# Other staging buffers for two weight pieces and for the half results, ahead of the second half of an output projection

## The chip, the cores and the metric

The kernel runs on one core of one Trainium2 chip. A core has a matrix engine (PE in the profile, with its weight loads as PEld), a vector engine (DVE), a scalar engine (ACT), a general engine (POOL) and a synchronising engine (SP), which here only issues DMA transfers. Each engine works through its own list of instructions in order, and waits at the head of that list until what an instruction needs is there. The metric is the time of one execution in microseconds (us) of device time; lower is better. "t0" to "t7" and other short names below are mine; the kernel's own names are given beside them.

## The reference, cut to what matters

One layer, 1024 tokens of width 1024, in float32. Only the first sub-layer's end and the second's start matter here:

```python
y_ssm = s5_mixer(u, ...)                      # 1024 x 512
y_fox = forgetting_attention(q, k, v, ...)    # 1024 x 512, 8 heads of 64
y_mix = concatenate([rms_norm(y_ssm, ssm_out_g), rms_norm(y_fox, fox_out_g)], axis=-1)
x = x + rms_norm(y_mix @ w_out, mix_post_g)
h = rms_norm(x, xa_pre_g)
x = x + rms_norm(memory_cross_attention(h, mem_n, xa_wq, xa_wkv, xa_wo), xa_post_g)
```

The product with `w_out` has two halves: the rows that belong to `y_ssm` and the rows that belong to `y_fox`. The change lies where the second half is computed and added to the first.

## The kernel before, in words

All of the work is one program in which a scheduler sets the order: the instructions are written in program order, with priorities, and the framework's own timeline decides the final order on each engine. Tiles come from pools. A pool with the tag "a" has 2 buffers, "b" 2, "c" 3, "d" and "e" 1 each, `raw` 2, `whl` 3 (`BUFS`, line 193; lines 59 to 66). Each buffer holds 128 x 1024 floats (512 KB); `whl` and `slab` buffers hold a high and a low part. Buffers of a tag are handed out in turn, in program order, so a tile waits for the work on the tile that had its buffer before. Float32 products are made of three matmuls, of a high and a low part (`mm3`, lines 121 to 124); the parts come from `split` (line 113 on ACT makes the high part, line 115 or 117 on DVE the low one).

Around the change, in program order:

* **Attention heads.** The last unit of the attention is head 7. Its values are multiplied (L782, L783), its result `yt` is brought out by ACT (L789) and DVE (L790), split into `yf` (L113, L117), squared (L802) and added up on POOL (L803) into the tile "d"; a few tiny matmuls (L237) turn these sums into one number per token, from which DVE and ACT work out `r_f`, the factor of the norm of `y_fox` (L139 to L145).
* **First half of the projection.** It has been written to DRAM earlier (`t1_d`, shown as `t_d` in the profile).
* **The four pieces of the weights of the second half** (lines 1026 to 1032), 512 KB each: load (L1029) and split into a `slab` (L113, L115). I call them f0 to f3. All four are loaded into `raw` before, which has two buffers.
* **The loop over eight tiles of 128 tokens** (lines 1035 to 1057). Tile j loads 128 rows of `x` into a "c" buffer (L1038), loads the half results into a tile `t` by two transfers of 64 rows each (L1041; I call this tile tj and the two transfers its pair), and for each half of the columns: 12 matmuls into a PSUM bank `x` (L122 to L124; there are four such banks), then on DVE `t = bank * r_f + t` (L1048), on ACT the sums of squares (L1050), on POOL `t = t * g_mp` (L1052). The row `g_mp` is loaded into "d" (L952) once the sums of the heads have been read there. At the end of a tile come the norm (L1054, L139 to L145), `x1 = t * r + x` on DVE (L1056) and the store of x1 from POOL's queue (L1057).
* **Between these**, `build_a(1)` is stepped: it loads four pieces of the query weights (`in_wqT`, L158, I call them q0 to q3) into `raw`, splits them into `whl`, and multiplies them into PSUM banks `g` (L122 to L124 with `e` and `whl`).
* **Next stage** (lines 1204 to 1221): for each of four heads, values from DRAM are split into a "b" tile (L1209), two pieces of `wo` go through `raw` or "e" into `whl`, and 24 matmuls fill four banks, `g` for heads 0 and 2 and `x` for heads 1 and 3. The rest of the second sub-layer follows.

So SP's list holds all the loads, in one order; ACT's list holds splits that wait for loads, and bank evacuations; a load that is late holds up everything that stands behind its split.

The lines around the change in the kernel before:

```python
    BUFS = {"a": 2, "b": 2, "c": 3, "d": 1, "e": 1, "t2": 3, "yt": 2}
...
    for i in range(4):
        w = raw([P, D])
        sp.dma_start(out=w, in_=a["w_out_f"][i])
        hl = slab([P, 2, D])
        split(hl[:, 0], hl[:, 1], w)
        wo.append(hl)
...
        t = tt("aab"[j % 3])
```

Of the kernel before, what the change touches and what calls it, by code (L numbers as in the profile page):

```python
# [17 lines left out]
P = 128  # L18
S = 1024
D = 1024  # L20
# [32 lines left out]
def layer(ctx: ExitStack, tc: tile.TileContext, a, out):  # L53
# [15 lines left out]
    def slab(shape, dt=F32R):  # L69
        return slabp.tile(shape, dt, name="slab", tag="slab")  # L70
# [4 lines left out]
    def raw(shape):  # L75
        return rawp.tile(shape, F32, name="raw", tag="raw")
# [7 lines left out]
    def sm(n, name):  # L84
        return small.tile([P, n], F32, name=name, tag=name)
# [26 lines left out]
    def split(hi, lo, src, mul=None, lo_eng=None):  # L112
        first = act.activation(out=hi, in_=src, func=AF.Copy, scale=1.0 if mul is None else mul)  # L113
        if mul is None:
            (lo_eng or dve).tensor_tensor(out=lo, in0=src, in1=hi.bitcast(F32), op=ALU.subtract)  # L115
        else:
            dve.scalar_tensor_tensor(out=lo, in0=src, scalar=mul, in1=hi.bitcast(F32),  # L117
                                     op0=ALU.mult, op1=ALU.subtract)
        return first

    def mm3(ps, lh, ll, rh, rl, first, last):
        pe.matmul(ps, lh, rh, start=first, stop=False)  # L122
        pe.matmul(ps, lh, rl, start=False, stop=False)  # L123
        pe.matmul(ps, ll, rh, start=False, stop=last)  # L124
# [70 lines left out]
    def tt(tag, shape=None, dt=F32):  # L195
        return t4.tile(shape or [P, S], dt, name=tag, tag=tag, bufs=BUFS[tag])
# [671 lines left out]
    def step(g, n=1):  # L868
        for _ in range(n):
            if next(g, "end") == "end":  # L870
                return
# [151 lines left out]
    def x_ps(shape):  # L1023
        return psx.tile(shape, F32, name="x", tag="x")

    wo = []
    for i in range(4):
        w = raw([P, D])
        sp.dma_start(out=w, in_=a["w_out_f"][i])  # L1029
        hl = slab([P, 2, D])  # L1030
        split(hl[:, 0], hl[:, 1], w)
        wo.append(hl)
    g_mp = gain_row(0, "d")
    a1 = build_a(1)
    for j in range(NT):
        ts = slice(j * P, (j + 1) * P)
        xt = tt("c")
        sp.dma_start(out=xt, in_=a["x"][ts, :])  # L1038
        t = tt("aab"[j % 3])
        for i in range(2):  # L1040
            sp.dma_start(out=t[64 * i:64 * i + 64], in_=t1_d.rearrange("j (k s) d -> s k j d", s=16)[2 * j + i])  # L1041
        ss4, ss, r = sm(4, "ss4"), sm(1, "ss"), sm(1, "r")
        for h in range(2):
            hs = slice(h * 512, h * 512 + 512)
            ps = x_ps([P, 512])
            for k in range(4):
                mm3(ps, yf[k][:, 0, ts], yf[k][:, 1, ts], wo[k][:, 0, hs], wo[k][:, 1, hs], k == 0, k == 3)
            dve.scalar_tensor_tensor(out=t[:, hs], in0=ps, scalar=r_f[:, j:j + 1], in1=t[:, hs], op0=ALU.mult, op1=ALU.add)  # L1048
            for q in range(2 * h, 2 * h + 2):
                act.activation(out=tt("yt", [P, 256]), in_=t[:, q * 256:q * 256 + 256], func=AF.Square,  # L1050
                               accum_out=ss4[:, q:q + 1])
            pool.tensor_tensor(out=t[:, hs], in0=t[:, hs], in1=g_mp[:, hs], op=ALU.mult)  # L1052
            step(a1)
        dve.tensor_reduce(out=ss, in_=ss4, op=ALU.add, axis=mybir.AxisListType.X)  # L1054
        rsqrt_mean(r, ss, D)
        dve.scalar_tensor_tensor(out=xt, in0=t, scalar=r, in1=xt, op0=ALU.mult, op1=ALU.add)  # L1056
        stC.dma_start(out=x1_d[j], in_=xt)  # L1057
# [249 lines left out]
    def ev():  # L1307
        return evp.tile([P, 512], F32, name="ev", tag="ev")
# [111 lines left out]
    for n in range(2):  # L1420
        w = ev()
# [185 lines left out]
```

## Time and profile before

| | |
|---|---|
| median of 3 runs | 1432.37 us (1430.96 to 1433.04) |
| the profiled execution's own time | 1430.57 us |
| its span, first to last instruction | 1428.8 us |
| mean granted clock of the matrix engine | 0.992 |
| PE busy | 1390.7 us (97%) |
| DVE, ACT, POOL busy | 1003.7, 708.0, 410.9 us |
| span from 475 to 585 us | PE busy 97.9 of 110 us |
| span from 585 us to the end | PE busy 834 of 843 us |

The profiled execution took 1.8 us more than its span and 1.8 us less than the median. The stretch of the change lies between about 475 and 585 us of the span, where PE is idle for 12 of 110 us; after it, it is idle for 9 of 843 us. In the timelines, a row has the start in us, the length in us, the engine, the line, the operation with output and input tiles, a count, and in brackets the idle time of the engine ahead of it with what ended it. SPq is SP's list, where a row is the issuing of a transfer, not the transfer. The names there come without numbers: `t_d` in `a<-t_d` is `t1_d`.

### The profile page before, as it was taken

The numbers are of one execution on the slowest core, as the hardware profiler recorded it, in microseconds if no ns is written. First come the engines' busy times: TensorE is split into PE (matmuls) and PEld (weight loads), VectorE is DVE, ScalarE is ACT, GpSimd is POOL, SyncE is SP. The second block draws the span as 40 slices with busy tenths as digits, with TensorE's granted clock in tenths as the row PEclk, the third lists the DMA queues.
The fourth block names the chain that finished last, engine by engine and source line by source line (L and its number), as shares of the span: only waits on it lengthen the run. The fifth ranks groups of instructions, "written<-read, shape, count | busy, mean of one in ns | idle before, by whom it ended". The sixth has DMA issues, their size and how long they took to land.

```text
span 1428.8 us, 20846 instructions
## 1 busy us (share of the span) xinstructions
PE 1390.7 (97%) x7422; PEld 1187.5 (83%) x7422; DVE 1003.7 (70%) x1818; ACT 708.0 (50%) x1421; POOL 410.9 (29%) x432
## 2 busy tenths in 40 slices
PE   7999999999999898999999999999999999999997
PEld 6889898889989886788888788888888888888886
DVE  7839947877888876645557677887766676565565
ACT  6373347777888754543434533333333334444341
POOL 0001000022243134001111367676666661000021
PEclk9999999999999999999999999999999999999999
DMA  6325654165654658323637455454444446965444
GB/s 204 98 80 148 183 192 132 33 204 178 193 153 120 172 164 276 134 74 109 193 112 236 149 190 173 168 181 154 164 156 162 162 155 227 334 219 192 177 162 162
DMA packets 112824, 238.43 MB, mean 167 GB/s; under 512 B 11848, under 2 KB 48712, under 8 KB 112592
## 3 DMA queue, kind: packets, MB, share of 16 engines
q1 hardware_dynamic: 96576, 182.01, 39.8%
q0 software_dynamic: 16144, 55.09, 10.6%
q8 instruction: 58, 0.95, 0.3%
q14 instruction: 46, 0.38, 0.1%
HBM read 168.90 MB, written 76.81 MB: 172 GB/s over the span
## 4 chain that ended last, share of the span: by engine, by line
PE 58%; DVE 1%; DMA 1%; ACT 0%; issue 0%; DVEq 0%; SPq 0%; ACTq 0%
PE x L1277 17%; PE g L1277 13%; PE x L1535 7%; PE g L1535 7%; PE x L123 2%; PE x L124 2%; PE x L122 2%; PE g L122 2%; PE g L124 2%; PE g L123 2%; PE g L1065 1%; DMA a<-t_d 1%; PE g L1173 1%; DVE slab L115 0%; DVE whl L115 0%; DVE c L1056 0%
## 5 line engine op out<-in xcount | busy, mean ns | idle before, releaser
L1277 PE MATMUL x<-slab,op 128*128 128x512 f32 x984 | 233.3, 389 | 0.5 <-DVE op L115 0.5
L1277 PEld LDWEIGHTS x<-slab,op 128*128 128x128 f32 x984 | 184.6, 188 | 39.3 <-DVE op L115 1.0
L1277 PE MATMUL g<-slab,op 128*128 128x512 f32 x744 | 178.7, 389 | 0.0
L115 DVE TENSOR_TENSOR slab<-slab 128x1024 fp32r<-128x1024 f32 (+2 forms) x92 | 110.2, 1207 | 84.7 <-ACT slab L113 82.8
L1277 PEld LDWEIGHTS g<-slab,op 128*128 128x128 f32 x744 | 139.6, 188 | 29.0
L122 PE MATMUL g<-slab,whl 128*128 128x512 f32 (+1 forms) x416 | 151.7, 365 | 0.6 <-ACT whl L113 0.4
L123 PE MATMUL g<-slab,whl 128*128 128x512 f32 (+1 forms) x416 | 148.4, 357 | 0.0
L124 PE MATMUL g<-slab,whl 128*128 128x512 f32 (+1 forms) x416 | 148.2, 357 | 0.0
L113 ACT ACTIVATE slab<-slab 128x1024 fp32r<-128x1024 f32 (+2 forms) x92 | 94.8, 1037 | 106.4 <-DMA slab<-hs_d 81.5
L1535 PE MATMUL g<-slab 128*128 128x512 f32 x462 | 126.6, 389 | 0.0
L1535 PE MATMUL x<-slab 128*128 128x512 f32 x462 | 126.6, 389 | 0.0
L1535 PEld LDWEIGHTS g<-slab 128*128 128x128 f32 x462 | 86.7, 188 | 18.0
L1535 PEld LDWEIGHTS x<-slab 128*128 128x128 f32 x462 | 86.7, 188 | 18.0
L122 PE MATMUL g<-whl,slab 128*128 128x256 f32 (+2 forms) x288 | 87.5, 309 | 9.6 <-ACT whl L113 7.3
L115 DVE TENSOR_TENSOR op<-slab,op 128x512 fp32r<-128x512 f32 x80 | 83.9, 1059 | 11.6 <-ACT op L113 11.3
L1353 POOL TENSOR_TENSOR wt<-wt 128x256 f32<-128x256 f32 x88 | 84.2, 957 | 19.9 <-DMA wt<-in_w_down 16.3
L113 ACT ACTIVATE op<-slab 128x512 fp32r<-128x512 f32 x80 | 50.0, 627 | 77.7 <-PE x L1277 37.5
L122 PEld LDWEIGHTS g<-slab,whl 128*128 128x128 f32 x416 | 78.6, 189 | 11.8 <-ACT whl L113 0.6
L124 PEld LDWEIGHTS g<-slab,whl 128*128 128x128 f32 x416 | 78.4, 189 | 11.6 <-DVE whl L115 0.2
L115 DVE TENSOR_TENSOR whl<-raw,whl 128x1024 fp32r<-128x1024 f32 (+2 forms) x61 | 72.0, 1184 | 22.3 <-ACT whl L113 21.7
L123 PEld LDWEIGHTS g<-slab,whl 128*128 128x128 f32 x416 | 78.6, 189 | 10.6
L123 PE MATMUL g<-whl,slab 128*128 128x256 f32 (+2 forms) x288 | 86.1, 299 | 0.0
(394 smaller groups left out, 3149.3 us busy)
## 6 DMA issues: line engine op xcount, KB each, us to landing
hs_d<-ev POOLq DMA_DIRECT2D x77, 256.0 KB, 2.6
slab<-hs_d SPq DMA_DIRECT2D x35, 512.0 KB
wt<-in_w_down SPq DMA_DIRECT2D x44, 256.0 KB
wt_d<-wt POOLq DMA_DIRECT2D x22, 512.0 KB, 4.8
slab<-in_w_gate SPq DMA_DIRECT2D x20, 512.0 KB
slab<-in_w_up SPq DMA_DIRECT2D x20, 512.0 KB
slab<-wt_d SPq DMA_DIRECT2D x20, 512.0 KB
wd_d<-in_w_down SPq DMA_DIRECT2D x33, 256.0 KB
```

The lines of the kernel that those rows point to most:

```text
L113: first = act.activation(out=hi, in_=src, func=AF.Copy, scale=1.0 if mul is None else mul)
L115: (lo_eng or dve).tensor_tensor(out=lo, in0=src, in1=hi.bitcast(F32), op=ALU.subtract)
L122: pe.matmul(ps, lh, rh, start=first, stop=False)
L123: pe.matmul(ps, lh, rl, start=False, stop=False)
L124: pe.matmul(ps, ll, rh, start=False, stop=last)
L1065: pe.transpose(tp[:, k], src[:, (k0 + k) * P:(k0 + k + 1) * P], ident)
L1173: turned = pe.transpose(tp[:, k], h3[:, (4 * n + k) * P:(4 * n + k + 1) * P], ident)
L1277: pe.matmul(ps, x[:, k], y[:, k], start=first and k + n == 0, stop=k == 3 and n == 2, skip_group_check=not first)
L1353: pool.tensor_tensor(out=o, in0=x, in1=y, op=ALU.subtract)
L1535: pe.matmul(banks[n][j], xo[:, u, js], wo[:, v], start=ends[0] and k == 0, stop=ends[1] and k == 2, skip_group_check=onto is not None)
```

## The change

Two edits. The third and the fourth piece (f2, f3) are loaded into one "a" and one "c" buffer in place of `raw`. And the tiles t0 to t7 take their buffers in the turn b, a, a in place of a, a, b:

```diff
     for i in range(4):
-        w = raw([P, D])
+        w = raw([P, D]) if i < 2 else tt("ac"[i - 2])
         sp.dma_start(out=w, in_=a["w_out_f"][i])
...
-        t = tt("aab"[j % 3])
+        t = tt("baa"[j % 3])
```

So before, t2 and t5 are in "b"; now t0, t3 and t6 are. No instruction is added or removed, and every tile, shape and sum is as before; but the scheduler puts the instructions of this stretch in another order on all engines.

SP's list, before, from the load of t5 (`b_6391`) to the load of q3 (`raw_6172`); `a_6046` is t1, `raw_5922` and `raw_5927` are f2 and f3, `c_...<-in_x` are rows of x, `raw_5970`, `raw_5975`, `raw_6167` and `raw_6172` are q0 to q3:

```order
L1041 DMA b_6391<-t1_d_112 64x1x1024 x2
L1038 DMA c_5934<-in_x 128x1024
L1038 DMA c_6044<-in_x 128x1024
L1041 DMA a_6046<-t1_d_112 64x1x1024 x2
L1029 DMA raw_5922<-in_w_out_f 128x1024
L1029 DMA raw_5927<-in_w_out_f 128x1024
L1038 DMA c_6135<-in_x 128x1024
L158 DMA raw_5970<-in_wqT 128x1024
L158 DMA raw_5975<-in_wqT 128x1024
L158 DMA raw_6167<-in_wqT 128x1024
L158 DMA raw_6172<-in_wqT 128x1024
```

The same place now; `b_6243` is t3, `a_6046` t1, `a_6137` t2 (f2 has been issued further up, in the place where t0's pair stood before):

```order
L1041 DMA b_6243<-t1_d_112 64x1x1024 x2
L1029 DMA c_5927<-in_w_out_f 128x1024
L1038 DMA c_5934<-in_x 128x1024
L1041 DMA a_6046<-t1_d_112 64x1x1024 x2
L158 DMA raw_5970<-in_wqT 128x1024
L158 DMA raw_5975<-in_wqT 128x1024
L1041 DMA a_6137<-t1_d_112 64x1x1024 x2
L1038 DMA c_6044<-in_x 128x1024
L1038 DMA c_6135<-in_x 128x1024
L158 DMA raw_6167<-in_wqT 128x1024
L158 DMA raw_6172<-in_wqT 128x1024
```

The first two q pieces have taken the place of f2 and f3, and the third, `raw_6167`, now stands behind the pair of t2 and two transfers of x rows.

ACT's list, before, from the split of f2 to that of q2; `g_5858` is the last bank of turned weights of head 7, `yt_5882` the last result of head 7:

```order
L113 ACTIVATE slab_5924<-raw_5922 128x1024
L113 ACTIVATE slab_5799<-g_5858 128x4x128
L113 ACTIVATE slab_5929<-raw_5927 128x1024
L113 ACTIVATE whl_5971<-raw_5970 128x1024
L789 ACTIVATE yt_5882<-g_5865 64x256
L113 ACTIVATE whl_5976<-raw_5975 128x1024
L113 ACTIVATE slab_5250<-yt_5882,gains_98 64x256
L802 ACTIVATE yt_5882<-yt_5882 64x256
L113 ACTIVATE whl_6168<-raw_6167 128x1024
```

The same place now, from the split of f3 on (that of f2 stands two rows ahead of it); `yt_5844` is the result before the last:

```order
L113 ACTIVATE slab_5929<-c_5927 128x1024
L789 ACTIVATE yt_5844<-g_5831 64x256
L113 ACTIVATE slab_5799<-g_5851 128x4x128
L113 ACTIVATE whl_5971<-raw_5970 128x1024
L113 ACTIVATE slab_5477<-g_5814,gains_98 128x256
L113 ACTIVATE slab_5799<-g_5858 128x4x128
L113 ACTIVATE whl_5976<-raw_5975 128x1024
L113 ACTIVATE slab_5250<-yt_5844,gains_98 64x256
L802 ACTIVATE yt_5844<-yt_5844 64x256
L113 ACTIVATE whl_6168<-raw_6167 128x1024
L789 ACTIVATE yt_5882<-g_5865 64x256
L113 ACTIVATE slab_5250<-yt_5882,gains_98 64x256
```

The split of q2 (`whl_6168`) stood behind the last result of head 7 and now stands ahead of it; the splits of f2 and f3 have moved ahead of everything that belongs to the last two results.

SP's list, before, further down, from t3 (`a_6243`) on; `a_6334` is t4, `a_6448` t6, `a_6505` t7, `e_6627` and `e_6683` are pieces of `wo`:

```order
L1041 DMA a_6243<-t1_d_112 64x1x1024 x2
L1041 DMA a_6334<-t1_d_112 64x1x1024 x2
L1038 DMA c_6241<-in_x 128x1024
L1208 DMA t2_6739<-kv_d_113 128x2x256
L158 DMA e_6627<-in_wo 128x1024
L1038 DMA c_6332<-in_x 128x1024
L158 DMA raw_6678<-in_wo 128x1024
L1038 DMA c_6389<-in_x 128x1024
L1041 DMA a_6448<-t1_d_112 64x1x1024 x2
L158 DMA e_6683<-in_wo 128x1024
L1038 DMA c_6446<-in_x 128x1024
L1041 DMA a_6505<-t1_d_112 64x1x1024 x2
```

The same place now; `b_6448` is t6, `a_6334` t4, `a_6391` t5, `a_6505` t7:

```order
L1041 DMA b_6448<-t1_d_112 64x1x1024 x2
L1041 DMA a_6334<-t1_d_112 64x1x1024 x2
L1038 DMA c_6241<-in_x 128x1024
L1041 DMA a_6391<-t1_d_112 64x1x1024 x2
L158 DMA e_6627<-in_wo 128x1024
L1038 DMA c_6332<-in_x 128x1024
L158 DMA raw_6678<-in_wo 128x1024
L1038 DMA c_6389<-in_x 128x1024
L1208 DMA t2_6739<-kv_d_113 128x2x256
L158 DMA e_6683<-in_wo 128x1024
L1041 DMA a_6505<-t1_d_112 64x1x1024 x2
L1038 DMA c_6446<-in_x 128x1024
```

Before, four pairs were still to be loaded from here on (t3, t4, t6, t7); now it is four as well (t6, t4, t5, t7), with t6 ahead of t4 and t5 ahead of `e_6627`.

## The prediction

> **What bounds the kernel now.** I read the page first: PE is busy for nearly all of the span, and the chain that ended last is mostly PE. A change that moves no work off PE can only change what PE loses to waits and to a slow clock, so I asked for the busy time in three stretches around the change (PE busy is the second number after the length, PEclk the granted clock):
>
> ```profile
> 475.00:530.00 55.00, 48.83 (x293) 43.42 (x292) 42.04 (x75) 35.56 (x85) 14.56 (x11) 0.94 0.58 173
> ...
> 530.00:585.00 55.00, 49.08 (x214) 38.36 (x214) 42.40 (x77) 31.14 (x87) 18.73 (x18) 0.94 0.82 271
> ...
> 585.00:1428.00 843.00, 834.05 (x3771) 690.92 (x3769) 548.53 (x796) 326.86 (x594) 299.05 (x315) 1.00 0.50 171
> ```
>
> PE is idle for 6.2 and 5.9 us in the two stretches of 55 us and for 9 us in all the 843 us behind them. So what is saved or lost before 585 us is neither caught up nor given back later; it goes into the end one for one. And no more than some 12 us of waiting is there to be saved. Single stretches of 10 us show where, and that the clock falls too:
>
> ```profile
> 500.00:510.00 10.00, 7.93 (x35) 6.41 (x35) 4.60 (x5) 4.96 (x6) 0.00 (x0) 0.83 0.47 157
> ...
> 540.00:550.00 10.00, 8.78 (x36) 6.60 (x36) 8.64 (x16) 6.21 (x19) 4.22 (x4) 1.00 0.95 306
> ...
> 570.00:580.00 10.00, 8.39 (x27) 6.33 (x28) 9.52 (x13) 9.54 (x19) 1.51 (x2) 0.69 0.90 312
> ```
>
> Next, who PE waited for from 440 to 620 us (total, times, longest):
>
> ```profile
> PE x L122 <- DVE a L1048: 3.7, 4, 1.4
> ...
> PE g L782 <- ACT slab L113: 2.0, 1, 2.0
> ...
> PE x L122 <- ACT whl L113: 1.7, 1, 1.7
> ```
>
> The group of the next stage's first matmuls on four `x` banks (head 1) has 2.1 of the 3.7 us, and the 1.7:
>
> ```profile
> L122 PE MATMUL x<-whl,b 128*128 128x512 f32 x16 | 6.1, 480 | 3.9 <-DVE a L1048 2.1 <-ACT whl L113 1.7
> ```
>
> So 1.6 us are left for the loop over tiles, and 2.0 for the attention's last values. In PE's timeline:
>
> ```profile
> 502.22 0.38 PE L782 MATMUL g<-slab 128*128 128x256 f32 x1 [1.97 <-ACT slab L113]
> ...
> 504.47 0.62 PE L123 MATMUL x<-slab 128*128 128x512 f32 x1
> ...
> 504.89 0.63 PE L124 MATMUL x<-slab 128*128 128x512 f32 x1
> ...
> 507.88 0.45 PE L122 MATMUL x<-slab 128*128 128x512 f32 x1
> ...
> 510.24 0.39 PE L123 MATMUL x<-slab 128*128 128x512 f32 x1
> ...
> 510.47 0.39 PE L124 MATMUL x<-slab 128*128 128x512 f32 x1
> ...
> 517.57 0.40 PE L122 MATMUL x<-slab 128*128 128x512 f32 x1
> ...
> 564.00 0.39 PE L122 MATMUL x<-whl,b 128*128 128x512 f32 x1
> ...
> 573.69 0.80 PE L123 MATMUL x<-whl,b 128*128 128x512 f32 x1 [0.29 <-DVE whl L115]
> ```
>
> PE waits 1.97 us at 502.22 for a split that stands in ACT's list behind the split of f2. Behind that wait, matmuls start 0.42 us apart (504.47 to 504.89) where 0.23 is normal (510.24 to 510.47), until 507.88: some 2 us more. Head 1's matmuls begin at 564.00; the tiny wait at 573.69 ends their 3.9 us of waits and 0.3 more, and from there on PE runs almost without a gap. So the place that counts is 573.69, and what releases it. The chain of waits names that:
>
> ```profile
> 557.35 7.99 DMA a<-t_d
> ```
>
> This is t7's pair, which can only be loaded when t4 has left its "a" buffer. From its landing the path runs over DVE, ACT and DVE to the matmuls at 573.69.
>
> **The change part by part.** Nothing is added or removed, so the sum is of shifts along this path. I follow it from the front.
>
> *f2 and f3 out of `raw`.* Loads and ACT's waits for them:
>
> ```profile
> 490.96 1.23 SPq L1041 DMA_DIRECT2D a<-t_d  x2
> ...
> 492.42 1.86 SPq L1029 DMA_DIRECT2D raw<-in_w_out_f  x2
> ...
> 502.97 8.67 SPq L158 DMA_DIRECT2D raw<-in_wqT  x4
> ```
>
> ```profile
> 500.63 1.06 ACT L113 ACTIVATE slab<-raw 128x1024 fp32r<-128x1024 f32 x1 [4.83 <-DMA raw<-in_w_out_f]
> ...
> 506.55 1.06 ACT L113 ACTIVATE whl<-raw 128x1024 fp32r<-128x1024 f32 x1 [3.43 <-DMA raw<-in_wqT]
> ...
> 507.63 0.38 ACT L789 ACTIVATE yt<-g 64x256 f32<-64x256 f32 x1
> ```
>
> f2, issued at 492.42 as soon as a `raw` buffer was free, landed 8.2 us later, because t1's pair stood ahead of it; q0, issued at 502.97 into an empty queue, took 3.6 us. The pair therefore costs up to 4.6 us in the queue. The other bound is its size: 512 KB at 306 GB/s, the rate from 540 to 550 us, is 1.7 us. I take 4.5, the row that shows a pair ahead of another load, and 1.7 for any whole 512 KB load.
>
> Now f2 goes out where t0's first half did, and f3 where the first x rows did, so both are split by about 495 us: the 4.83 us of ACT at 500.63 go, as far as they belong to f2. But q0 and q1 take f2's and f3's buffers, places and so landing times: q0 at 500.6, with the split of the last turned bank behind it as before, and PE gets that bank about when it did. The new thing is q2. It is issued at about 503 as q0 was, but behind q1, t2's pair and two x loads. Five loads of 512 KB from 500.6 on at 306 GB/s end at 509.2; with 4.6 for the pair and 1.7 for the four others, at 512.0; with an empty queue at 506.5. I take 510, since the fastest stretch had pairs in it too. In ACT's list q2's split (1.06) now stands ahead of L789, so head 7's last result comes out at 511.1 instead of 507.63, 3.5 us later. Queued behind it are L113, L802, all evacuations of the four `g` banks, and by them PE.
>
> *r_f and the first tiles.*
>
> ```profile
> 516.49 1.41 DVE L1048 SCALAR_TENSOR_TENSOR a<-x,r_f,a 128x512 f32<-128x512 f32 x2
> ...
> 528.67 2.21 DVE L1056 SCALAR_TENSOR_TENSOR c<-a,r,c 128x1024 f32<-128x1024 f32 x1
> ```
>
> ```profile
> 519.80 7.50 POOL L1052 TENSOR_TENSOR a<-a,d 128x512 f32<-128x512 f32 x4 [7.93 <-DMA d<-in_post_g]
> ```
>
> From L789 to the first L1048 it took 8.9 us, with two q splits of over 1 us on the way; one of them is now past. I take 7.6: L1048 at 518.7 instead of 516.49, 2.2 later (bounds: 1.3 earlier, with q2 at 506.5, and 4.5 later, with 512.0 and 8.9). PE's third tile began at 517.57 without a wait; now it needs the bank that L1048 frees at 519.4. So PE's gain of 1.97 us and some 2 us of slow clock is spent here, on the wait for L789's bank and for L1048, and 1.8 us more.
>
> On POOL the first product with the row `g_mp` waited for that row:
>
> ```profile
> 515.15 0.38 SPq L952 DMA_DIRECT2D d<-in_post_g  x1
> ...
> 530.90 3.37 SPq L1041 DMA_DIRECT2D a<-t_d  x4
> ...
> 549.58 1.23 SPq L1041 DMA_DIRECT2D a<-t_d  x2
> ...
> 556.71 1.23 SPq L1041 DMA_DIRECT2D a<-t_d  x2
> ```
>
> The row is issued at about the same time (the sums come some 2 us later, but SP's list got to it some 2 us after them before). POOL now waits instead for ACT's squares, which come after two splits of 1.06 us and two short ones, some 0.9 together, that cannot start before 518. With 0.9 for the squares of a half that makes 521.9. It needs 7.5 us for four halves, so t0's two are ready at 525.7, before DVE comes to its L1056 (528.67 before; I take 529.1, as the splits that stood ahead of it between the L1048 are fewer now). This hides the 2.2 us almost wholly: the pair of t6 goes out at 531.2, where that of t3 went at 530.90, and t4's at 533.7, 1.0 later than before (last two of the row at 530.90).
>
> *t3 in "b".* It has landed long ago, and DVE's waits of 3.80 and 1.14 us for pairs change:
>
> ```profile
> 539.55 0.75 DVE L1048 SCALAR_TENSOR_TENSOR a<-x,r_f,a 128x512 f32<-128x512 f32 x1 [3.80 <-DMA a<-t_d]
> ...
> 545.35 0.75 DVE L1048 SCALAR_TENSOR_TENSOR a<-x,r_f,a 128x512 f32<-128x512 f32 x1 [1.14 <-DMA a<-t_d]
> ...
> 555.40 1.28 DVE L1056 SCALAR_TENSOR_TENSOR c<-a,r,c 128x1024 f32<-128x1024 f32 x1
> ...
> 565.46 0.75 DVE L1048 SCALAR_TENSOR_TENSOR a<-x,r_f,a 128x512 f32<-128x512 f32 x1 [3.11 <-DMA a<-t_d]
> ...
> 572.42 1.22 DVE L115 TENSOR_TENSOR whl<-raw,whl 128x1024 fp32r<-128x1024 f32 x1
> ```
>
> ```profile
> 548.56 1.06 ACT L113 ACTIVATE whl<-e 128x1024 fp32r<-128x1024 f32 x1 [1.51 <-DMA e<-in_wo]
> ```
>
> ```profile
> 568.66 0.92 ACT yt L1050 x4
> ```
>
> The wait at 539.55 was for t3 and goes, and with it at most the 1.6 us of PE's waits; PE is 1.8 us late by then. What is late next is t4: it was the fourth half from the first issue, 14.4 us behind it, and is so again, at 545.7; the x1 stores go out up to 2 us later and share the engines with it, so I take 546.3, 0.9 later. Then t5, which was loaded into "b" ahead of all this, is now loaded behind t4 and an x load: 1.7 + 4.5 gives 552.5, and the `wo` piece in "e" behind it 554.2, where ACT had it at 548.56. In both lists these stand ahead of t4's end: on DVE t5's first L1048, on ACT the split of that piece, ahead of t4's Ln and Exp. From there 1.06 (split), some 1.2 (its low part on DVE) and 0.7 (the norm): t4's L1056 at 557.1 instead of 555.40, 1.7 later. Bounds: 1.5 earlier, if a pair costs 2 us, to 4 later, if stores fall in between.
>
> *t7.* Its pair goes out when that L1056 is done, at 558.4 (before 556.71). It landed 8.7 us behind its issue, with a `wo` piece and an x load ahead; the x load now stands behind it, which saves 1.7, and a store beside it costs about 1: 566.2 against 565.46, 0.7 later. From the landing to the low part at 572.42 nothing changes but the split of head 1's values: they now wait for t6's "b" buffer and stand between t7's L1048 and its norm. ACT does that while DVE works on L1048, and DVE while ACT squares, so it costs 0 to 0.7; I take 0.3. PE's 12 matmuls on these values ran while it waited, from 564 on; now they start at about 569.5 and take 2.7 us, 5.2 at the slow clock, and end before 574.7, when the low part is there. That wait is their cover; without it they would cost those 2.7 us.
>
> **Sum.** 0.7 + 0.3 = 1.0 us later at 573.69 and at the end. The profiled execution took 1430.57, so it would take 1431.6; it lies 1.8 below the median, 1432.37, so I forecast 1433.4. Its own bounds are about -1.5 and +2.5 us. A measurement of this kernel tells about 0.2% (2.9 us) from no change, so this counts as the same.
>
> **Rivals.** *Pairs are cheap (faster).* If a pair costs near its lower bound, some 2 us and not 4.5, q2 is there by 507, L1048 comes 1 us earlier, t5 lands at about 549, the piece in "e" at 550.7, t4's L1056 is at 553.5, and t7's pair lands at 562, 3.5 us earlier; then the tail gains 3.5 us: 1428.9. For it speaks that the removed waits are real (1.97 and 3.80 us) and that four of eight tiles are now there in time; against it the 8.2 us of f2. The Trainium skill, "DMA: Bandwidth & Descriptors", section "Why a DMA increments its semaphore by 16 and not by 1", says that a transfer uses the largest number of engines up to 16 that divides both slowest dimensions; here 8 rows by 8, so 8 engines, and at the 27 GiB/s per engine of its section Specifications 512 KB take an estimated 2.3 us. By that the sum would be this rival's; no row here shows the number of engines, and f2's 8.2 us speak for a dearer pair.
>
> *t5 drags t4 (slower).* The pair of t5 and the "e" piece now stand in front of t4's norm, in a stretch where transfers already run at 95% busy. If the three x1 stores, now later, fall between them, t5 lands after 554.5 and not at 552.5. From that point each microsecond goes on to t4's L1056, t7's pair and the end: with 560 for L1056 t7 lands at 569, 3.5 later, with the inserted split 3.8: 1436.2. For it speaks the DMA share of 0.95 from 540 on; against it that SP has one x load less ahead of t7.
>
> *It does nothing.* The same eight pairs go through the same queue, and t7 hangs on t4 and t1 as before; if the queue alone sets t7, the end is within 1 us of now, 1432.4. This lies in the forecast's own range.
>
> **How the numbers follow.** Forecast with "does nothing" 0.45, cheap pairs 0.29, t5 drags t4 0.26. These are the chances of same, faster and slower. The forecast alone spans 1430.9 to 1435.9; to leave out no more than 2 in 10, the range goes past the two rivals' times by a little over 1 us: 1427.5 to 1437.2.
>
> **What would show it.** Right: ACT idle until about 510 ahead of q2's split; L789 of the last result past 510.5; the first L1048 at 518 to 519.5; no wait of DVE at 539; t4's L1056 at 556 to 558.5; the chain still through t7's pair, landing at 565 to 567.5. Wrong: q2's split by 507.5, or t4's L1056 before 554 or after 559.5, or a chain that passes another transfer.

## The result, and the profile after

The changed kernel took 1433.05 us (median of 12 runs, 1432.09 to 1438.43). The kernel before, run beside it, took 1431.21 (1427.21 to 1433.04). The ratio is 1.0022 with a 95% interval of 1.0012 to 1.0031, that is 3.1 us slower (1.7 to 4.4), just at the 0.2% that the prediction took as the bound of "the same". It isn't the quotient of the two medians, which lie 1.8 us apart (the means lie 3.5 apart). Four runs in all (one of the kernel before, beside the changed one, and one each in three of the sets below) took 300 us and more longer than the rest; the medians here count them, the ranges and the ratios leave them out. The forecast of 1433.4 us is met within 0.4 us, but as a difference it was too small: it said 1.0 us. That the two agree so well is luck: the three runs of before that it started from, which are among the twelve here, had a median of 1432.37, 1.2 above that of the twelve. The profiled execution of the changed kernel took 1432.44 us, with a span of 1430.7 and a mean granted clock of 0.992.

Time marks of two profiles can't be set against each other as they stand. PE's timeline of before has a wait of 2.30 us early in the stretch, ahead of all that the change moves on PE, and near the stretch's end the first matmuls of head 3 on `x` banks, with that head's first piece of `wo` (head 1's 24 matmuls begin at 564.00, head 2's at 576.81):

```profile
478.46 0.39 PE L122 MATMUL g<-a,whl 128*128 128x256 f32 x1 [2.30 <-DVE slab L117]
...
582.25 1.07 PE L122 MATMUL x<-whl,b 128*128 128x512 f32 x4
```

The same rows of the changed kernel's timeline, with what PE waited for between them:

```profile
477.05 0.58 PE L122 MATMUL g<-a,whl 128*128 128x256 f32 x1 [2.30 <-DVE slab L117]
...
502.72 0.39 PE L783 MATMUL g<-slab 128*128 128x256 f32 x1 [0.90 <-DVE slab L115]
...
517.92 0.50 PE L122 MATMUL x<-slab 128*128 128x512 f32 x1 [1.52 <-DVE b L1048]
...
568.92 0.50 PE L122 MATMUL x<-whl,b 128*128 128x512 f32 x1 [0.36 <-ACT b L113]
...
574.01 0.50 PE L123 MATMUL x<-whl,b 128*128 128x512 f32 x1 [0.61 <-DVE whl L115]
...
583.60 1.19 PE L122 MATMUL x<-whl,b 128*128 128x512 f32 x4 [1.54 <-ACT whl L113]
```

The changed kernel came to the 2.30 us wait 1.4 us earlier than before, and was as much earlier already at 462.03, where it loads the first piece f0 (463.43 before), ahead of the first load that the change moves: this is how far two runs can differ. So I call this wait the **reference row** and measure from it. From there to the end before took 1428.8 - 478.46 = 950.3 us, the changed kernel 953.6, 3.3 more, near the 3.1 of the timed runs. And most of the difference arises within the stretch: from the last row of each fence to the end it is 846.6 us before and 847.1 after, and between 846.1 and 847.8 in every profile below. As the forecast said, what is lost here isn't given back; a microsecond more or less behind the stretch tells nothing.

The same windows as before, for the front and for the rest of the span:

```profile
585.00:1428.00 843.00, 835.92 (x3776) 691.99 (x3776) 545.25 (x798) 328.69 (x597) 294.37 (x315) 1.00 0.50 171
...
500.00:510.00 10.00, 8.87 (x50) 8.36 (x49) 5.24 (x6) 4.68 (x8) 0.79 (x1) 0.70 0.57 201
```

PE's wait of 1.97 us for head 7's values at 502.22 has become one of 0.90 at 502.72; but the clock in these ten microseconds is 0.70 where it was 0.83. What follows on ACT's list:

```profile
507.94 1.06 ACT L113 ACTIVATE whl<-raw 128x1024 fp32r<-128x1024 f32 x1 [4.21 <-DMA raw<-in_wqT]
509.03 0.38 ACT L789 ACTIVATE yt<-g 64x256 f32<-64x256 f32 x1
...
552.73 1.06 ACT L113 ACTIVATE whl<-e 128x1024 fp32r<-128x1024 f32 x1 [1.36 <-DMA e<-in_wo]
```

q2's split stands ahead of head 7's last result and keeps it 4.21 us waiting; the piece of `wo` in "e" is split at 552.73 where it was 548.56. DVE's list:

```profile
517.12 1.41 DVE L1048 SCALAR_TENSOR_TENSOR b<-x,r_f,b 128x512 f32<-128x512 f32 x2
...
527.38 1.22 DVE L145 SCALAR_TENSOR_TENSOR r<-rst,rsy 128x1 f32<-128x1 f32 x1
528.52 1.33 DVE L141 SCALAR_TENSOR_TENSOR rst<-rsy,rsv 128x1 f32<-128x1 f32 x1
529.77 1.27 DVE L1056 SCALAR_TENSOR_TENSOR c<-b,r,c 128x1024 f32<-128x1024 f32 x1
...
545.50 0.75 DVE L1048 SCALAR_TENSOR_TENSOR a<-x,r_f,a 128x512 f32<-128x512 f32 x1 [4.95 <-DMA a<-t_d]
...
547.76 1.93 DVE L1056 SCALAR_TENSOR_TENSOR c<-b,r,c 128x1024 f32<-128x1024 f32 x1 [0.93 <-DMA c<-in_x]
...
555.21 1.22 DVE L145 SCALAR_TENSOR_TENSOR r<-rst,rsy 128x1 f32<-128x1 f32 x1
556.52 1.28 DVE L1056 SCALAR_TENSOR_TENSOR c<-a,r,c 128x1024 f32<-128x1024 f32 x1
```

The wait for t3's pair at 539 is gone, and one of 4.95 us for t4's pair stands in its place. The row at 547.76 waits for rows of `x`, as none of this group did before. The chain of waits still ends over t7's pair, and has the piece in "e" ahead of it, at 13 us from issue to landing:

```profile
539.74 12.97 DMA e<-in_wo
...
558.47 7.18 DMA a<-t_d
```

### The profile page after: what moved, and what is told of

Its sections match the earlier page's. It is cut to its first block, busy times and chain, and to the rows that moved or that the text cites. A ratio compares the mean times of both kernels' runs of the same rounds, so it can differ in the third digit from the quotient of the medians.

```text
span 1430.7 us, 20850 instructions
## 1 busy us (share of the span) xinstructions
PE 1392.1 (97%) x7422; PEld 1188.9 (83%) x7422; DVE 1001.1 (70%) x1818; ACT 707.7 (49%) x1421; POOL 405.5 (28%) x432
## 4 chain that ended last, share of the span: by engine, by line
PE 86%; DVE 5%; ACT 4%; DMA 3%; issue 1%; SPq 0%; POOL 0%; DVEq 0%; ACTq 0%; POOLq 0%
PE x L1277 17%; PE g L1277 13%; PE g L122 8%; PE g L124 8%; PE g L123 8%; PE x L1535 7%; PE g L1535 7%; PE x L124 2%; PE x L123 2%; PE x L122 2%; PE g L771 2%; ACT slab L113 1%; DMA raw<-in_wqT 1%; PE g L1065 1%; DMA e<-in_wo 1%
## 5 line engine op out<-in xcount | busy, mean ns | idle before, releaser
L115 DVE TENSOR_TENSOR slab<-slab 128x1024 fp32r<-128x1024 f32 (+2 forms) x92 | 110.0, 1204 | 84.7 <-ACT slab L113 82.6
L113 ACT ACTIVATE slab<-slab 128x1024 fp32r<-128x1024 f32 (+2 forms) x92 | 95.2, 1037 | 105.0 <-DMA slab<-hs_d 77.3
L115 DVE TENSOR_TENSOR op<-slab,op 128x512 fp32r<-128x512 f32 x80 | 83.8, 1058 | 11.2 <-ACT op L113 10.8
L115 DVE TENSOR_TENSOR whl<-raw,whl 128x1024 fp32r<-128x1024 f32 (+2 forms) x61 | 71.7, 1180 | 27.5 <-ACT whl L113 27.0
L123 PEld LDWEIGHTS g<-slab,whl 128*128 128x128 f32 x416 | 78.7, 189 | 10.7
L1353 POOL TENSOR_TENSOR wt<-wt 128x256 f32<-128x256 f32 x88 | 81.1, 921 | 19.9 <-DMA wt<-in_w_down 16.5
## 6 DMA issues: line engine op xcount, KB each, us to landing
slab<-hs_d SPq DMA_DIRECT2D x35, 512.0 KB
wt_d<-wt POOLq DMA_DIRECT2D x22, 512.0 KB, 5.0
slab<-in_w_gate SPq DMA_DIRECT2D x20, 512.0 KB
slab<-in_w_up SPq DMA_DIRECT2D x20, 512.0 KB
slab<-wt_d SPq DMA_DIRECT2D x20, 512.0 KB
```

The costliest lines, as they stand in the source:

```text
L1353: pool.tensor_tensor(out=o, in0=x, in1=y, op=ALU.subtract)
```

## The experiments

They ran in three sets, each on one chip beside runs of before (medians 1430.72, 1430.81 and 1432.16 us). Ratios are to those, with 95% intervals. My first theory was that the turn of the buffers costs the time: t5 and the piece in "e" now stand ahead of t4's norm and drag it (the second rival of the prediction, at part of its size). The rival theory was the front: q2's split holds head 7's last result, and everything behind it is that much later. Both took it that a pair is dear in the queue.

**The changed kernel again**

> The changed kernel once more, beside the others of this set and with a second profile. If the loss of about 3 us is real and not chance, it is again 2 to 5 us slower than before; PE again waits for the split of a piece of wo near 583 us (1.54 us in the first profile after the change), because t6's store again takes over 5 us. If that wait was chance of one run, it is absent here and the rest of the loss stays at about 1.7 us.

It took 1435.09 us, 1.0032 (1.0020 to 1.0045), so the loss is real. PE's timeline of this run, then DVE's, then the chain of waits:

```profile
477.14 0.39 PE L122 MATMUL g<-a,whl 128*128 128x256 f32 x1 [2.30 <-DVE slab L117]
...
576.72 0.50 PE L123 MATMUL x<-whl,b 128*128 128x512 f32 x1 [0.60 <-DVE whl L115]
...
585.30 1.20 PE L122 MATMUL x<-whl,b 128*128 128x512 f32 x4 [0.55 <-ACT whl L113]
```

```profile
527.23 1.21 DVE L145 SCALAR_TENSOR_TENSOR r<-rst,rsy 128x1 f32<-128x1 f32 x1
...
529.61 2.40 DVE L1056 SCALAR_TENSOR_TENSOR c<-b,r,c 128x1024 f32<-128x1024 f32 x1
...
557.60 1.22 DVE L145 SCALAR_TENSOR_TENSOR r<-rst,rsy 128x1 f32<-128x1 f32 x1
...
558.90 1.28 DVE L1056 SCALAR_TENSOR_TENSOR c<-a,r,c 128x1024 f32<-128x1024 f32 x1
```

```profile
541.91 13.19 DMA e<-in_wo
...
560.85 7.53 DMA a<-t_d
```

The shape is that of the first profile, but more is lost up to the place that the prediction followed: 576.72 - 477.14 = 99.58 us, where the first took 574.01 - 477.05 = 96.96 and before 573.69 - 478.46 = 95.23. In the first profile, another 1.1 us went behind that place, in the wait of 1.54 us at 583.60; here that wait is 0.55, and nothing more is lost. Two profiles of one kernel thus split the loss differently, 1.7 first and the rest later against 4.35 at once.

The matmuls of 583.60 wait for the split of head 3's first piece of `wo`, which is loaded into `raw`. In SP's list of the changed kernel its load stands directly behind a load of x1 (L1075) that waits until the store of t6's x1 has landed: the store was issued at 569.29, the load of x1 at 575.08, the piece at 575.50. That is 98.5 us behind the reference row, 3.3 later than before (573.66, as soon as its buffer was free); in the repeat it is 101.1 (578.19), 5.9 later. So what is lost behind the place of 573.69 need not be chance. It isn't shown either: in the repeat the chain of waits names the landing of this piece (578.19, 5.89 us), in the first profile a tiny operation of DVE, and no run changes this order alone.

**The staging alone, and the turn alone.** The first undoes the changed turn, the second the staging:

```diff
-        t = tt("baa"[j % 3])
+        t = tt("aab"[j % 3])
```

> Only the staging: f2 and f3 in the buffers a and c, tiles in the turn a, a, b as before. This has the first loads of the changed kernel (q2 behind two more loads and ahead of the last L789) with the later loads of the kernel before (t5 early in b). Theory 1 (the turn costs it: t5 is loaded behind t4, its x1 is stored late, and that store meets t6's): at most 1 us slower than before, t5's store issued by 562.5, no PE wait over 0.5 us at 583. Theory 2 (the front costs it: q2's split ahead of L789 and all that follows): about the whole loss, 2.5 to 3.5 us slower.

```diff
-        w = raw([P, D]) if i < 2 else tt("ac"[i - 2])
+        w = raw([P, D])
```

> Only the turn b, a, a; f2 and f3 in raw as before. First loads of the kernel before, with PE's wait of some 2 us for f2 at 502, but later loads of the changed kernel. Theory 1: 2 to 4 us slower than before, t5's store at 564 to 566 and a PE wait over 1 us at 583. Theory 2: within 1 us of before, as q2 is where it was.

The staging alone took 1431.72, 1.0008 (0.9999 to 1.0017), the turn alone 1431.17, 1.0003 (0.9993 to 1.0012): neither alone makes a difference that this measurement shows. Neither theory holds as a sole cause. The two halves together cost 3.1 and 4.6 us, one by one 1.1 and 0.4; as the intervals of the halves reach to 2.4 and 1.7 us, it is likely rather than certain that together they cost more than the sum. With the staging alone, in the timelines of PE and ACT:

```profile
479.75 0.58 PE L122 MATMUL g<-a,whl 128*128 128x256 f32 x1 [2.30 <-DVE slab L117]
...
574.89 0.79 PE L123 MATMUL x<-whl,b 128*128 128x512 f32 x1 [0.30 <-DVE whl L115]
...
583.95 1.07 PE L122 MATMUL x<-whl,b 128*128 128x512 f32 x4
```

```profile
550.13 1.06 ACT L113 ACTIVATE whl<-e 128x1024 fp32r<-128x1024 f32 x1 [0.53 <-DMA e<-in_wo]
```

With the turn alone, PE, DVE and ACT:

```profile
478.07 0.39 PE L122 MATMUL g<-a,whl 128*128 128x256 f32 x1 [2.30 <-DVE slab L117]
...
582.29 1.07 PE L122 MATMUL x<-whl,b 128*128 128x512 f32 x4
```

```profile
548.99 1.28 DVE L1056 SCALAR_TENSOR_TENSOR c<-b,r,c 128x1024 f32<-128x1024 f32 x1 [3.85 <-DMA c<-in_x]
...
571.73 1.23 DVE L115 TENSOR_TENSOR whl<-raw,whl 128x1024 fp32r<-128x1024 f32 x1 [1.12 <-ACT whl L113]
...
576.00 1.28 DVE L1056 SCALAR_TENSOR_TENSOR c<-a,r,c 128x1024 f32<-128x1024 f32 x1
```

```profile
552.20 1.06 ACT L113 ACTIVATE whl<-e 128x1024 fp32r<-128x1024 f32 x1 [0.26 <-DMA e<-in_wo]
```

All marks from the reference row on, in us; before as a time, the others as what they come later (+) or earlier than it:

| | before | forecast | changed | changed again | staging alone | turn alone |
|---|---|---|---|---|---|---|
| head 7's last L789 begins | 29.2 | +3.5 | +2.8 | +3.7 | +3.0 | -0.7 |
| first L1048 begins | 38.0 | +2.2 | +2.0 | +2.9 | +2.2 | -0.6 |
| t0's x1 done (L1056) | 52.4 | +0.4 | +1.6 | +2.4 | +1.7 | -0.5 |
| t4's pair landed | 66.8 | +0.9 | +1.6 | +3.4 | - | -1.2 |
| piece in "e" landed | 70.1 | +5.6 | +5.6 | +7.9 | +0.3 | +4.0 |
| t4's x1 done | 78.2 | +1.7 | +2.5 | +4.8 | -2.2 | +1.5 |
| t7's pair landed | 86.9 | +0.7 | +1.7 | +4.4 | 0.0 | +2.2 |
| the place of 573.69 | 95.2 | +1.0 | +1.7 | +4.4 | -0.1 | - |
| head 3's first x4 matmuls (582.25) | 103.8 | - | +2.8 | +4.4 | +0.4 | +0.4 |
| end | 950.3 | +1.0 | +3.3 | +4.3 | -0.1 | +1.0 |

The staging makes the front 1.7 us later alone, and 1.6 and 2.4 in the changed kernel. Alone this goes no further: t5 was loaded early into "b", the piece in "e" is there at 70.4, and t4's x1 even comes 2.2 us earlier than before. The turn alone brings the piece in "e" 4.0 us later, behind t5's pair, but on a front that is half a microsecond early. In the first profile of the changed kernel the two add up, 4.0 + 1.6 to the 5.6 by which the piece is late; in the repeat they don't, 4.0 + 2.4 against 7.9. How a late front gets there is in the chain of waits of the first profile: t0's x1 is stored, the store frees a "c" buffer, and the load of `x` into that buffer is what SP's list has ahead of t5's pair and the piece in "e":

```profile
531.34 6.64 DMA x_d<-c
...
538.00 0.33 SPq L1038
```

So I read the loss thus: the turn uses up the slack that swallowed the late front. Up to t4 the table fits that. Behind t4 it doesn't: with the turn alone t7's pair lands 2.2 us late, later than in the first profile of the changed kernel (1.7), and yet head 3's first matmuls begin only 0.4 late. The two rows of DVE above give a reason. With the turn alone, the low part of the piece of `wo` that head 1's matmuls need (571.73, 93.7 us behind the reference row) stands ahead of t7's x1 (576.00). Before and in the changed kernel it stands behind it: 572.42 behind 571.22, and 572.74 behind 571.54 (95.7 us). So the turn alone may cost nothing because its lists have another order there, and not because slack is left. That rival isn't ruled out: no run is the changed kernel with this one split ahead of t7's x1.

**t5 in "b" again, t4 last of the "a" run.** The changed kernel with another turn, so that t5 is no longer loaded behind t4:

```diff
-        t = tt("baa"[j % 3])
+        t = tt("baaaabaa"[j])
```

> The changed kernel with another turn, b, a, a, a, a, b, a, a: t0 and t5 in b, so t5 is loaded early again and the first two pieces of the next stage's weights stand where they did; t3 is late instead. Theory 1: the loss goes but for at most 1 us; no PE wait over 0.5 us at 583. Theory 2: the loss stays, 2.5 to 3.5 us, as the front is that of the changed kernel.

It took 1436.92, 1.0041 (1.0028 to 1.0053): slower still, and outside what either theory gave. SP's list and then the chain of waits:

```profile
540.20 0.35 SPq L1038 DMA_DIRECT2D c<-in_x  x1
540.65 1.22 SPq L1041 DMA_DIRECT2D a<-t_d  x2
```

```profile
541.28 13.50 DMA a<-t_d
```

t4's pair now stands behind a load of `x` that waits for the store of t0's x1 (its "c" buffer), and lands 75.9 us behind the reference row (478.86 in this run), 9.1 later than before. So t5 behind t4 isn't needed for a loss. It fits that whatever stands behind a load that hangs on the late front costs; the edit moves other loads too, so it doesn't show that alone. The profile is of the slowest of the five runs.

**Half results by one load of 128 rows each.** On the kernel before and on the changed kernel:

```diff
-        for i in range(2):
-            sp.dma_start(out=t[64 * i:64 * i + 64], in_=t1_d.rearrange("j (k s) d -> s k j d", s=16)[2 * j + i])
+        sp.dma_start(out=t, in_=t1_d.rearrange("j p d -> (j p) d")[ts, :])
```

In these two kernels the tiles get half results of other tokens; the number of bytes, the matmuls and the rest of the work stay.

> The kernel before, with each tile of half results loaded by one transfer of 128 rows that lie one behind the other in DRAM, in place of a pair of 64 rows each; so a tile gets the half results of other tokens. This takes out the price of the pair alone; all engines' lists stay as they were. If a pair costs 4.5 us in the queue and a plain 512 KB load 1.2 to 1.7: f2 lands some 3 us earlier and PE's 2 us wait for it at 502 goes, t3 and t4 are there in time, t7 lands 2 to 3 us earlier: 4 to 7 us faster than before. If a pair costs about 2 us: within 1 us of before.

> The changed kernel with the same plain loads of 128 rows, so also with half results of other tokens. Theory 1 and 2 have it in common that transfers which stand behind pairs (q2 in front, the piece of wo in e and t5 later) make the change lose: then with plain loads the loss goes, and this kernel is within 1 us of the kernel before with plain loads, or faster than it. If the loss has nothing to do with pairs, this kernel is 3 to 4.5 us slower than that one, as the changed kernel is than before.

They took 1420.63, 0.9925 (0.9912 to 0.9938), and 1422.88, 0.9944 (0.9932 to 0.9956). PE's timelines at the matmuls of 582.25, of the kernel before with plain loads and of the changed kernel with plain loads:

```profile
573.21 1.20 PE L122 MATMUL x<-whl,b 128*128 128x512 f32 x4 [0.86 <-ACT whl L113]
```

```profile
576.56 1.20 PE L122 MATMUL x<-whl,b 128*128 128x512 f32 x4 [1.34 <-ACT whl L113]
```

With the reference rows at 480.37 and 481.80 these are 92.8 and 94.8 us behind them, where before had 103.8. By the ratio, the pairs cost the kernel before 10.7 us, more than the 4 to 7 expected. The edit takes out two things at once, the second transfer and the order of the rows (a pair picks eight times eight rows at a stride, a plain load takes rows that lie one behind the other); which of them costs isn't separated. The prediction's first rival had pairs at 2 us where any load takes 1.7, 0.3 more each and 2.4 in all: they are not nearly so cheap. But that price isn't the whole of what the change loses: with cheap loads the changed kernel is still behind, 2.2 us by the medians and 1.9 by these two rows. The two intervals just touch, but each of its five runs (1422.01 to 1424.89) is slower than each of the other four (1420.07 to 1421.59). This lies between the two expectations: what both theories had in common fell as the sole cause. DVE's list of the changed kernel with plain loads shows the wait that has taken the pairs' place:

```profile
544.28 1.28 DVE L1055 SCALAR_TENSOR_TENSOR c<-b,r,c 128x1024 f32<-128x1024 f32 x1 [2.19 <-DMA c<-in_x]
```

It is for rows of `x`, which stand behind another tile's load in SP's list. The turn alone has the same wait, of 3.85 us (548.99). The Trainium skill, "SBUF — State Buffer", section "Can I just issue two DMAs to hit both halves?", says that two transfers of half the partitions serialize and that only one transfer over all 128 partitions uses all ports; the 10.7 us agree in sign, and no run here times one pair by itself.

**q2 behind the last squares.** q2's split is ordered to come after head 7's last squares (L802), once on the changed kernel and once on the staging alone:

```diff
+            wq = [load_w(..., behind=last_sq[0] if hd == 3 else None) for d in range(2)]
...
-                with tc.high_priority(offset=boost):
+                with tc.high_priority(offset=boost), (tc.issue_after(behind.ins) if behind else ExitStack()):
```

> The changed kernel with ACT's splits of q2 and q3 put behind the last L802 of head 7, where q2's stood before the change; the loads are as in the changed kernel but for t5's pair, which now goes ahead of an x load, and one piece of wo, which goes ahead of an x1 load. Theory 2 (the front): the last L789 comes some 2 us earlier and most of the 3 to 4.5 us goes, within 1.5 us of before. Theory 1 (the later loads): 2 to 4 us slower than before, as the changed kernel. With both needed for the loss, as the two halves of the change alone suggest (1.1 and 0.4 us against 3.1 to 4.6 together): 0 to 1.5 us slower.

> Only the staging, with the turn a, a, b, and with the splits of q2 and q3 put behind the last L802. The front now gains PE's wait of 2 us for f2 and gives nothing back at L789. If that gain reaches the end, 1 to 3 us faster than before; if the pairs of t3, t4 and t7 set the end whatever the front does, as the staging alone suggests (its loop began 1.4 us later, measured from 475 us, and it ended as before), within 1 us of before.

They took 1434.42, 1.0014 (1.0001 to 1.0027), and 1431.66, 1.0004 (0.9991 to 1.0017). The first is 2.0 us slower than before by the ratio, not the 0 to 1.5 expected if both halves are needed. It did what it was to do at the front: the last L789 begins at 503.11, 25.8 us behind the reference row (477.30), 3.4 earlier than before and 6.2 earlier than in the changed kernel. The gain was eaten behind it. DVE's list and PE's timeline of that run:

```profile
564.27 1.97 DVE L1057 SCALAR_TENSOR_TENSOR c<-b,r,c 128x1024 f32<-128x1024 f32 x1 [1.38 <-DMA c<-in_x]
```

```profile
566.96 0.80 PE L122 MATMUL x<-whl,b 128*128 128x512 f32 x1 [5.43 <-ACT b L113]
```

This is t6: its rows of `x` stand behind t7's pair, its x1 is late, so its "b" buffer is free late, and head 1's values are split into that buffer. PE waits for them, 5.43 us. The profile shown is of the fastest of these runs (1428.76 to 1436.24), and from the reference row to its end it took 949.7 us, 0.6 less than before; so it gives the way in which the gain is lost rather than the size of the loss. On the staging alone the edit changes nothing that can be told (1431.66 against 1431.72), as a kernel that swallows the late front should.

**Norms ahead.** Four kernels try to win back single steps. The first lets t2's squares on ACT wait for t0's norm; the second puts the split of the piece in "e" behind t4's norm and x1; the third does both; the fourth does the second on the kernel before, as a control:

```diff
-                act.activation(out=tt("yt", [P, 256]), in_=t[:, q * 256:q * 256 + 256], func=AF.Square,
+                with tc.issue_after(norms[0].ins) if j == 2 else ExitStack():
+                    act.activation(out=tt("yt", [P, 256]), in_=t[:, q * 256:q * 256 + 256], func=AF.Square,
```

> The changed kernel with the squares of tile t2 put behind the norm of t0 on ACT; nothing else is put elsewhere by hand. Theory 3 is that the late front goes on to the end since everything behind it hangs on t0's norm and store: in the changed kernel t0's L1056 came 1.1 us later than before (529.77 against 528.67) though the forecast had 0.4, as t0's Ln and Exp stand behind a square of t2. If that hand-over is on the path, t0's L1056 comes 1 to 2 us earlier here and the end 1 to 2 us earlier than in the changed kernel, so 1.5 to 2.5 us slower than before. If not, it stays 3 to 4.5 us slower.

```diff
+                with tc.high_priority(offset=boost), ExitStack() as stack:
+                    for b in behind:
+                        stack.enter_context(tc.issue_after(b.ins))
...
+        wo_ = [load_w(..., behind=(norms[4], x1s[4]) if h == 1 and d == 0 else ()) for d in range(2)]
```

> The changed kernel with the split of the piece of wo in e (both parts) put behind t4's norm and L1056; t7's pair then also stands ahead of the second piece in e. In both profiles of the changed kernel t4's L1056 came 3.8 us behind the landing of that piece (556.52 behind 552.70, 558.90 behind 555.09). The forecast's step, that this landing sets t4's norm and with it t7's pair: t4's L1056 at 552 to 554, t7's pair issued 3 to 5 us earlier, the end 2 to 4 us earlier than in the changed kernel, so from 1 us faster to 2 us slower than before. If the loss comes from elsewhere, it stays 3 to 4.5 us slower.

> Both edits together on the changed kernel. If each works on its own part of the one path, 0 to 3 us faster than before, as nothing of the changed kernel's loss is left and PE's wait for f2 stays removed; if t7's pair is held by the full queue instead, 1 to 2 us slower than before.

> The kernel before with the second edit alone: the split of the piece in e behind t4's norm and L1056. There the piece lands at 548.54, 7 us ahead of t4's L1056 at 555.40, so it does not hold t4 up: within 1 us of before. If it is 2 us faster or more, the edit is worth something by itself, and a gain of the same edit on the changed kernel tells nothing of the change.

They took 1436.83, 1.0038 (1.0023 to 1.0053); 1435.89, 1.0030 (1.0020 to 1.0040); 1434.15, 1.0018 (1.0006 to 1.0030); and 1432.68, 1.0004 (0.9992 to 1.0016). None gains. The first tells nothing: t0's L1056 begins 53.1 us behind the reference row, no earlier than in the changed kernel (52.7), so the step that it was to win back wasn't won; here too PE waits at head 1's values, 4.13 us. The second did its job: t4's x1 is done 80.1 us behind the reference row (481.39), 0.6 and 2.9 earlier than in the two runs of the changed kernel. Yet its end is no earlier. The profile is of the slowest of its runs (1433.52 to 1438.75). DVE's list and PE's timeline show what PE waited for instead:

```profile
573.60 1.92 DVE L1059 SCALAR_TENSOR_TENSOR c<-b,r,c 128x1024 f32<-128x1024 f32 x1 [1.43 <-DMA c<-in_x]
```

```profile
576.24 0.50 PE L122 MATMUL x<-whl,b 128*128 128x512 f32 x1 [3.32 <-ACT b L113]
```

It is the way over t6 again: rows of `x`, x1, the "b" buffer, head 1's values. With both edits PE waits 2.55 us at the same matmul. With the staging alone, the chain of waits itself passes t6's rows of `x`, behind a store, and not t7's pair:

```profile
551.86 8.88 DMA x_d<-c
560.75 6.94 DMA c<-in_x
```

So right behind the way over t7's pair lies a second one over t6's rows of `x`, and a gain on the first shows up as a wait on the second. Apart from the two with plain loads, no kernel here beat the kernel before. A version with plain loads and the right half results would need them written to DRAM in another layout; it wasn't tried.

## Why the prediction was right or wrong

**What bounds, and no give-back: right.** The loss lies between the reference row and head 3's first matmuls, as far as the rest lets one tell, which takes 846.1 to 847.8 us in every profile.

**f2 and f3 out of `raw`, q2 late: right in way and size.** L789 was forecast 3.5 us later and came 2.8 and 3.7 later. By their times the first three signs of "what would show it" were missed (q2's split at 507.94, L789 at 509.03, the first L1048 at 517.12), since that run had reached the stretch 1.4 us early.

**PE's gain at the front: not seen.** The wait fell from 1.97 to 0.90 us, and the clock in that window was lower, not higher. It would have been spent on the wait for L1048 anyway, as forecast: 1.52 us at 517.92. In the repeat the wait is 0.36, and PE then waits 3.38 us at 511.72 for head 7's last result.

**First L1048: right** (+2.2 forecast, +2.0 and +2.9). Its upper bound was added up wrongly: 512.0, the split of 1.06 and 8.9 give 522.0, 5.5 later and not 4.5. (So was t7's landing, by 0.2: 558.4 + 8.7 - 1.7 + 1 is 566.4. Neither decides anything here.)

**"This hides the 2.2 us almost wholly": wrong, and the step that failed.** I forecast t0's x1 0.4 us later; it was 1.6 and 2.4 later. The time between the first L1048 and the end of t0's x1 has two parts. Up to t0's L145, the last operation of its norm, fewer splits on DVE were to give back 1.8 us: before it took 527.76 - 516.49 = 11.27 us, in the first profile 527.38 - 517.12 = 10.26, in the repeat 527.23 - 518.07 = 9.16, so 1.0 and 2.1 came back. From L145 to the end of L1056 nothing was to change: before it took 530.88 - 527.76 = 3.12 us, then 531.04 - 527.38 = 3.66 and 532.01 - 527.23 = 4.78, so 0.5 and 1.7 were lost. The row of before:

```profile
527.76 0.80 DVE L145 SCALAR_TENSOR_TENSOR r<-rst,rsy 128x1 f32<-128x1 f32 x1
```

What differs is which DVE operations ran beside POOL's products and lasted longer for it. In the first profile these are two splits of weights (L115, 3.45 us at 519.76 where the repeat has 2.35), L145 and t1's L141 (1.22 and 1.33); in the repeat L145, L141 and t0's L1056 (2.40 where it else takes 1.27); before, L145 (0.80) and L1056 (2.21). POOL's list of the changed kernel there and at t4's norm:

```profile
524.32 5.52 POOL L1052 TENSOR_TENSOR a<-a,d 128x512 f32<-128x512 f32 x4
...
555.13 1.28 POOL L1052 TENSOR_TENSOR a<-a,d 128x512 f32<-128x512 f32 x1 [2.40 <-DVE whl L115]
```

I had t0's two products ready at 525.7 (they were at 524.4) and counted only whether they were ready, not what POOL's products do to DVE.

**t3 in "b": right.** There is no wait at 539. The piece in "e" is 5.6 us late in the first profile, as forecast, but by luck: t4's pair was 0.7 later than forecast, and the piece landed 7.3 us behind that pair where the forecast had 7.9.

**t4's x1, t7's pair, the place of 573.69: right in the way, too small.** +1.7, +0.7 and +1.0 were forecast, +2.5, +1.7 and +1.7 came in the first profile, +4.8, +4.4 and +4.4 in the second. t4's L1056 begins within "556 to 558.5" in the first and just past it in the second. In the first profile, what was too small is the term for t4's norm. From the landing of the piece in "e" to t4's L1056 the forecast has 2.9 us (1.06, 1.2 and 0.7); both profiles have 3.8 (552.70 to 556.52, 555.09 to 558.90), as L145 took 1.22 us beside POOL's product (555.21, and 557.60 in the repeat). So the same oversight costs 0.9 us a second time. In the repeat the piece itself landed 2.3 us later than forecast, near the 2.0 by which t0's x1 was later than forecast, on the way over the store shown above. This second profile lies between the forecast and the rival "t5 drags t4". That rival named the right place and way; its cause, stores that fall ahead of t5, isn't shown by any run.

**The inserted split, 0 to 0.7 us: right for the changed kernel** (PE waits 0.36 us for it at 568.92, 0.64 in the repeat, and its matmuls end before the low part is there; from t7's landing to the place of 573.69 it took 8.36 and 8.34 us, before 8.35, so the 0.3 weren't needed). But its price was read as if t7's path were alone. The experiments show the path over t6's rows of `x` close behind, and that I hadn't priced.

**The number.** As a difference the forecast was 2 us short; its own bounds, -1.5 to +2.5, hold only the lower part of the measured interval (1.7 to 4.4). In the first profile 0.7 of these 2 us are there at the place of 573.69, which is t4's norm less the 0.3 of the inserted split; 1.1 come at 583.60, where head 3's first piece of `wo` goes out late; the rest lies within the scatter of what follows. In the repeat nearly all of it is there at the place of 573.69. That both halves are needed for the loss is likely; why the turn alone doesn't lose stays open.

## What to carry to other kernels

Two edits that each cost nothing measurable can cost something together, when one makes a front late and the other moves loads behind it: price the pair, with each late on top of the other, and ask for every moved load what it now stands behind. When a scheduler orders the lists, a run with half of a change has lists of its own; read them up to the end of the stretch before calling the halves independent. Ask also what runs beside each step of the path, not only what is ready for it. Look for the second path that lies right behind the critical one before you count on a gain. Profiles of two kernels are best compared from a row ahead of the change, and a difference that rests on three runs of before carries their scatter with it.

## What the runs showed of the hardware

* **Tiny DVE operations wait for POOL.** L145 on 128x1 takes 0.14 to 0.16 us when no product of POOL is under way. At 555.21 it took 1.22 and ended at 556.43; POOL's product, which began at 555.13, ended at 556.41. Where L145 began first, it wasn't held: in the kernel before it took 0.16 us at 547.11, and POOL's product began at 547.18. The Trainium skill, "SBUF — State Buffer", section "Who interferes with whom", says that a DVE instruction with two inputs in SBUF is blocked by a POOL instruction that reads there until that one ends; the rows agree, and show that it holds for an operation of one column.
* **Two transfers of 64 rows at a stride instead of one of 128 consecutive rows** cost 10.7 us over eight tiles (0.9925, 0.9912 to 0.9938), in a stretch where PE was idle for some 12 us in all.
* **The granted clock** was 0.83 from 500 to 510 us before, with one wait of 1.97 us; 0.70 in the first profile of the changed kernel, with waits of 0.90 and 0.16. In the repeat it was 1.00 there, with a wait of 0.36, and 0.66 from 510 to 520 us, with a wait of 3.38. What sets it isn't shown here.
* **Runs wander.** The reference row, ahead of what the edits move on PE, lies between 477.0 and 481.9 us in the fourteen profiles.
